# Hybrid mLSTM and stick-breaking layer: k's turned blocks sent by GpSimd, q's weight multiplied on landing, one more head with a longer way from split to product

## The chip, the cores and the metric

The kernel runs on one core of a Trainium2 chip. Times are device microseconds of one execution; several runs are made and their median is compared. The engines named below are PE (TensorE: matmuls), DVE (VectorE), ACT (ScalarE), POOL (GpSimd) and SP (SyncE, which here only issues DMAs). Each engine works through its own instructions in order, and an instruction that has to wait holds everything behind it on that engine.

## What is computed

One layer for 512 tokens of width 1024, in float32. The input is normalised and goes through one projection whose columns feed an mLSTM branch (4 heads of 256), a stick-breaking attention branch (8 heads of 128) and the gates; both branches are projected, merged and projected again.

```
h    = rmsnorm(x, norm_w)
proj = h @ w_in + b_in
mq, mk, mv, mi, mf, mo, mz, sq, sk, sv, sz, gates = split(proj)
hm   = mlstm_chunkwise(silu(conv(mq)), silu(conv(mk)), mv, mi, log_sigmoid(mf))
y_m  = rmsnorm(hm) * sigmoid(mo) * silu(mz)
y_s  = stick_breaking_attention(rmsnorm(sq), rmsnorm(sk), sv) * silu(sz)
x    = x + (g_m * (y_m @ w_proj_m) + g_s * (y_s @ w_proj_s)) @ w_out
```

The change lies in the stick-breaking branch. For a block of 128 queries, with z = q k / sqrt(128):

```
log_beta = log_sigmoid(z);  log_1mb = where(causal, log_sigmoid(-z), 0)
between  = reverse_cumsum(log_1mb) - log_1mb
a        = where(causal, exp(log_beta + between), 0)
out      = a @ v
```

## The kernel before

**Units.** The dense products are cut into 118 units; a unit is one piece of a weight of 128 x 1024 numbers and, in most, 24 matmuls of 512 columns. Each float32 operand is split into a high part (ACT copies it to a reduced format) and a low part (DVE subtracts, line 97), and three matmuls (lines 91 to 93) replace one. The main loop (line 1246) goes from unit to unit. In a unit c it runs what was put off to c (`defer`), evacuates the accumulator of unit c - 1, splits weights until two units ahead (`AHEAD`), issues half of the unit's matmuls (`mm(0)`), lets each active attention head take one step (`next(g)`), starts the heads that are due, and issues the other half (`mm(1)`). In the units in `REST` (11, 16, 20, 23, 24, 32, 44, 64) the active heads take no step. There is no scheduler: the order on every engine is the order in which this loop writes.

**The units around the change.** Set 1 of the stick-breaking heads has q in units 16 to 19, k in 20 to 23, z in 24 to 27, v in 28 to 31. The first mLSTM pair follows: its output gate in 32 to 35, its z in 36 to 39, its q and k with the convolution in 40 to 47, its v in 48 to 51. A v group fills four PSUM banks (`dps`), all that there are for dense units; unit 32 can begin once DVE has taken the first of them out (line 413). The z evacuation has two DVE instructions (690, 691), a convolution four (702, 704) with a sigmoid on ACT (707), a multiply (710) and a last subtraction (719).

**Turned blocks.** Where (q or k, set) stands in `TURNED`, the 32x32 blocks of the raw rows are transposed by DVE (`turn`, tile `ty`), and in the next unit 16 DMAs (`move`, line 399) put the blocks at their places (tile `tz`, one for each pair of heads). In set 1 every second one of the 16 is issued by POOL, the others by SP. q's rows are not scaled by its norm weight before; `head` multiplies the whole tile by the weight vector `qkw` (line 434) ahead of the split of each even head.

**A head** (`head`, line 424) is a generator; each `yield` ends a step. Step 1 splits q and k (`qtt`, `ktt`). Step 2 makes the scores of rows 3, 0 and 1 on PE and weighs rows 3 and 0: two sigmoids on ACT, two masks on POOL (463, 466), a scan and a product on DVE (469, 470). Step 3 makes the scores of row 2, transposes the blocks of rows 3 and 0 (487) and weighs rows 1 and 2. Step 4 transposes the rest. Steps 5 and 6 issue 8 DMAs each (line 506, by POOL in set 1) that put the blocks in place (`az`, two buffers). Step 7 is empty. Step 8 splits the first two columns of blocks (`ath`, `atl`: `turn((0,))`, `turn((1,))`), step 9 multiplies them with v (`apply`) and splits the other two (`turn((2, 3))`), step 10 multiplies these, step 11 multiplies the result by the gate (546). In set 1 the heads 2 and 3 take one empty step before each of the two products.

`SB_START` holds the unit in which each head takes its first step: 30, 33, 35 and 38 for set 1. So head 0 makes its scores in 31, head 2 in 36, head 3 in 39; head 0's last split stands in 39, head 1's in 41 with its product in 42.

Of the kernel before, what the change touches and what calls it, by code (L numbers as in the profile page):

```python
# [9 lines left out]
FR = mybir.dt.float32r  # L10
BF = mybir.dt.bfloat16
AF = mybir.ActivationFunctionType
OP = mybir.AluOpType
# [10 lines left out]

SB_START = [10, 13, 16, 19, 30, 33, 35, 38]
M_START = [52, 56, 70, 76]
GATES_PREP, GATES_START = 3, 4
TURNED = {("q", 0), ("q", 1), ("k", 1)}  # L30
# [5 lines left out]
def tile_hybrid_layer(  # L36
# [16 lines left out]
    nc = tc.nc  # L53
# [20 lines left out]
    def blk(tag, dt=F32, shape=(512,), name=None, p=128):  # L74

        where = mp if tag in MISC else sp
        return where.tile([p] + list(shape), dt, name=name or tag, tag=tag, bufs=BUFS[tag])

    def two(tag, dt=F32, name=None):

        t = blk(tag, dt, (2, 512), name=name)
        return t[:, 0, :], t[:, 1, :]
# [4 lines left out]
    def att_ps():  # L87
        return psa.tile([128, 512], F32, name="aps", tag="aps")
# [6 lines left out]
    def split(src, hi, lo):  # L95
        nc.scalar.activation(hi, src, AF.Copy)  # L96
        nc.vector.tensor_tensor(lo, src, hi.bitcast(F32), op=OP.subtract)  # L97
# [98 lines left out]
    def defer(n, fn):  # L196
        later.setdefault(now[0] + n, []).append(fn)
# [26 lines left out]
    qkw = cst.tile([128, 1], F32, name="qkw")  # L224
# [93 lines left out]
    class SbSet:  # L318
# [64 lines left out]
        def turn(self, name, g):  # L383

            ty = sp.tile([128, 8, TB, 32], F32, name="ty", tag="A", bufs=4)
            for tb in range(TB):
                nc.vector.transpose(ty[:, :, tb, :],
                                    self.raw[name][tb][:, 256 * g:256 * g + 256].rearrange("p (x j) -> p x j", j=32))  # L390

            def move():
                tz = blk("qk", F32, (2, 4, 128), name="tz")
                self.tz[name].append(tz)
                src = ty.rearrange("p (h b) i j -> p b h (i j)", h=2)
                for b in range(4):
                    for a in range(4):
                        q = nc.gpsimd if self.s and a % 2 else nc.sync
                        q.dma_start(tz[32 * b:32 * b + 32, :, a, :], src[32 * a:32 * a + 32, b])

            defer(1, move)
            if g == 0:
                defer(1 if name == "k" else 2, lambda: self.turn(name, 1))
            elif name == "k":
                defer(3, lambda: done.add(("k", self.s)))
# [18 lines left out]
        def head(self, h):  # L424
            hs = slice(h * 128, (h + 1) * 128)
            tr = []
            for name in ("q", "k"):
                th, tl = own = two("qk", FR, name=name + "tt")
                if (name, self.s) in TURNED:
                    tp = self.tz[name][h // 2][:, h % 2].rearrange("p a (i j) -> p i a j", j=32)  # L430
                    th, tl = [x.rearrange("p (i a j) -> p i a j", a=4, j=32) for x in own]
                    if name == "q" and h % 2 == 0:
                        z = self.tz[name][h // 2]
                        nc.vector.tensor_scalar(z, z, qkw, None, op0=OP.mult)
                else:
                    tp = att_ps()
                    for tb in range(TB):
                        nc.tensor.transpose(tp[:, tb * 128:(tb + 1) * 128], self.raw[name][tb][:, hs], ident)
                if name == "q" and not (name, self.s) in TURNED:
                    nc.scalar.activation(th, tp, AF.Copy, scale=qkw)  # L440
                    nc.vector.scalar_tensor_tensor(tl, tp, qkw, th.bitcast(F32), op0=OP.mult, op1=OP.subtract)
                else:
                    split(tp, th, tl)
                tr.append(own)
# [58 lines left out]
            for b in range(4):  # L503
                for a in range(4):
                    q = nc.gpsimd if self.s else nc.sync
# [9 lines left out]
            def turn(js):  # L515
                n0, n1 = slot[js[0], js[0]], slot[TB - 1, js[-1]] + 1
                at = (n1 - n0) * 128
                ah, al = blk("y", FR, name="ath"), blk("y", FR, name="atl")
                split(az[:, :, n0:n1, :].rearrange("p b i j -> p i b j"),
                      *[x[:, 0:at].rearrange("p (i b j) -> p i b j", b=4, j=32) for x in (ah, al)])  # L520
                for j in js:
                    o, n = (slot[j, j] - n0) * 128, T - j * 128
                    a_parts[j] = ah[:, o:o + n], al[:, o:o + n]

            turn((0,))
            turn((1,))
            yield
            if self.s and h >= 2:
                yield
            op = att_ps()  # L530

# [4 lines left out]
            apply(0)  # L536
            apply(1)
            turn((2, 3))
            yield
            if self.s and h >= 2:  # L540
                yield
            apply(2)
            apply(3)
# [1 line left out]
            y = y_s[4 * self.s + h]  # L545
# [668 lines left out]
    for s in (0, 1):  # L1214
        for h in range(4):
            pend.append((SB_START[4 * s + h], 1,
                         lambda s=s: ("k", s) in done, lambda s=s, h=h: sets[s].head(h)))
# [28 lines left out]
    for c in range(N):  # L1246
# [26 lines left out]
        for e in list(pend):  # L1273
            if c >= e[0] and e[2]():
                pend.remove(e)
                g = e[3]()
# [36 lines left out]
```

## Time and profile before

| what | value |
|---|---|
| median of 3 runs | 703.98 us (702.88 to 704.81) |
| profiled execution, its own time | 703.04 us |
| span of the profiled execution | 701.3 us |
| mean granted clock of TensorE over the span | 0.997 |
| POOL busy | 156.1 us, 22% |
| SP's queue (q1): share of 16 DMA engines | 37.0% |
| POOL's queue (q0): share of 16 DMA engines | 6.3% |

The page gives the busy time of each engine and its share of the span. A list of waits gives, for an engine, the instruction that waited and what it waited for. A timeline row has the start from the span's beginning, the duration, the engine, the line, the operation and its tiles, and in brackets the idle time of the engine before it with what ended that. A table by stretches has the stretch and its length, then the busy time and number of instructions of PE, of its weight loads, of DVE, ACT and POOL, then the granted clock of TensorE, the share of the DMA engines and GB/s. The matmuls are pipelined, so their durations overlap; their pace is read from start to start.

### The profile page before, as it was taken

Reading aid. Unit: us, or ns where it says so; the run is one execution under the profiler, and the core shown is the slowest. Engines: PE = TensorE matmul, PEld = TensorE weight load, DVE = VectorE, ACT = ScalarE, POOL = GpSimd, SP = SyncE. Lnnn points to the kernel's source line nnn. Section 1 sums busy time; section 2 is a strip of 40 time slices with the busy share of each in tenths; the row PEclk is TensorE's granted clock in tenths of the full one; section 3 lists DMA queues with packets and bytes.
Section 4 is the critical chain, followed back from the end, with each engine's and each line's share of the span. In section 5 each row is a group of like instructions: output and inputs, shape, how many; then the busy total and the mean of one; then the engine's idle time right before and its main releaser. Section 6 shows DMA issues by size and latency. Waiting matters only on the chain.

```text
span 701.3 us, 9357 instructions
## 1 busy us (share of the span) xinstructions
PE 688.5 (98%) x3172; PEld 571.2 (81%) x3172; DVE 472.9 (67%) x835; ACT 334.6 (48%) x629; POOL 156.1 (22%) x345
## 2 busy tenths in 40 slices
PE   7999999999999999899999999999999999999997
PEld 5888888788887788788888888888888888888886
DVE  6847997866847797998634638995444364445896
ACT  6244364565335554344365534447464353344451
POOL 5422132265602666400002020001111000111010
PEclk9999999999999999999999999999999999999999
DMA  7433524535553343333342244433323446589334
GB/s 246 136 89 103 164 71 125 142 84 164 147 162 91 98 128 98 101 90 104 90 100 82 60 104 125 118 91 90 91 61 83 113 150 225 140 171 225 127 80 131
DMA packets 109881, 84.11 MB, mean 120 GB/s; under 512 B 8302, under 2 KB 92680, under 8 KB 109832
## 3 DMA queue, kind: packets, MB, share of 16 engines
q1 hardware_dynamic: 104600, 73.93, 37.0%
q0 software_dynamic: 5088, 9.44, 6.3%
q8 instruction: 25, 0.41, 0.2%
q14 instruction: 24, 0.20, 0.1%
q10 hardware_dynamic: 144, 0.13, 0.1%
HBM read 65.12 MB, written 2.10 MB: 96 GB/s over the span
## 4 chain that ended last, share of the span: by engine, by line
PE 88%; DVE 5%; POOL 3%; DMA 1%; issue 1%; ACT 1%; SPq 1%; DVEq 0%; POOLq 0%; ACTq 0%
PE dps L91 25%; PE dps L93 25%; PE dps L92 25%; PE aps L92 3%; PE aps L93 3%; PE aps L91 2%; POOL az L506 1%; PE dps L1202 1%; DVE wl L97 1%; PE dps L1200 1%; PE dps L1201 1%; DMA stg<-in_w_in_dram 1%; PE aps L812 1%; PE aps L814 1%; DVE om L469 1%
## 5 line engine op out<-in xcount | busy, mean ns | idle before, releaser
L97 DVE TENSOR_TENSOR wl<-stg,wh 128x1024 fp32r<-128x1024 f32 x92 | 112.5, 1223 | 111.4 <-ACT wh L96 110.3
L91 PE MATMUL dps<-hh,wh 128*128 128x512 f32 x448 | 175.8, 392 | 1.3 <-DVE tmp L413 1.3
L93 PE MATMUL dps<-hh,wl 128*128 128x512 f32 x448 | 175.0, 391 | 0.0
L92 PE MATMUL dps<-hl,wh 128*128 128x512 f32 x448 | 174.9, 390 | 0.0
L96 ACT ACTIVATE wh<-stg 128x1024 fp32r<-128x1024 f32 x92 | 96.7, 1052 | 56.8 <-PE dps L93 28.0
L91 PEld LDWEIGHTS dps<-hh,wh 128*128 128x128 f32 x448 | 84.6, 189 | 18.3 <-DVE tmp L413 1.7
L93 PEld LDWEIGHTS dps<-hh,wl 128*128 128x128 f32 x448 | 84.4, 188 | 18.0
L92 PEld LDWEIGHTS dps<-hl,wh 128*128 128x128 f32 x448 | 84.5, 189 | 16.8
L91 PE MATMUL dps<-wh,hh 128*128 128x512 f32 x224 | 88.2, 394 | 0.4 <-DVE qraw L346 0.4
L93 PE MATMUL dps<-wh,hl 128*128 128x512 f32 x224 | 87.3, 390 | 0.0
L92 PE MATMUL dps<-wl,hh 128*128 128x512 f32 x224 | 87.3, 390 | 0.0
L91 PEld LDWEIGHTS dps<-wh,hh 128*128 128x128 f32 x224 | 42.1, 188 | 9.3 <-issue 0.8
L93 PEld LDWEIGHTS dps<-wh,hl 128*128 128x128 f32 x224 | 42.0, 188 | 9.0
L92 PEld LDWEIGHTS dps<-wl,hh 128*128 128x128 f32 x224 | 42.1, 188 | 8.2
L704 DVE SCALAR_TENSOR_TENSOR acc<-tmp,vec,acc 128x511 f32<-128x511 f32 (+2 forms) x48 | 36.0, 750 | 1.7
L707 ACT ACTIVATE tmp<-acc 128x512 f32<-128x512 f32 x16 | 10.1, 633 | 56.5 <-DVE acc L704 56.5
L463 POOL TENSOR_SCALAR_AFFINE_SELECT om<-om 128x128 f32<-128x128 f32 x32 | 17.3, 541 | 85.5 <-ACT om L461 85.5
L506 POOL DMA_DIRECT2D az<-ay x64 | 31.8, 504 | 19.7 <-ACT tmp L699 11.3
L469 DVE TENSOR_TENSOR_SCAN om<-om 128x512 f32<-128x512 f32 (+3 forms) x32 | 26.8, 836 | 9.2 <-POOL om L463 9.1
L125 POOL DMA_DIRECT2D wl<-stg x8 | 6.9, 868 | 93.7 <-DVE yml L97 61.7
L765 POOL TENSOR_SCALAR_AFFINE_SELECT w_all<-om 128x128 f32<-128x128 f32 x16 | 5.1, 351 | 91.7 <-DVE om L760 91.7
L461 ACT ACTIVATE om<-aps,rq 128x512 f32<-128x512 f32 (+3 forms) x32 | 16.8, 525 | 17.4 <-PE aps L93 16.5
(276 smaller groups left out, 1281.6 us busy)
## 6 DMA issues: line engine op xcount, KB each, us to landing
stg<-in_w_in_dram SPq DMA_DIRECT2D x87, 512.0 KB, 3.8
stg<-in_w_proj_s_dram SPq DMA_DIRECT2D x8, 512.0 KB, 3.9
B<-in_w_out_dram SPq DMA_DIRECT2D x8, 512.0 KB, 4.7
stg<-in_w_proj_m_dram SPq DMA_DIRECT2D x8, 512.0 KB, 3.7
wl<-stg POOLq DMA_DIRECT2D x8, 512.0 KB, 5.8
az<-ay SPq DMA_DIRECT2D x64, 40.0 KB, 2.7
az<-ay POOLq DMA_DIRECT2D x64, 40.0 KB, 1.8
brow<-in_b_in_dram SPq DMA_DIRECT2D x8, 256.0 KB, 5.5
```

The costliest lines, as they stand in the source:

```text
L91: nc.tensor.matmul(ps, ah, bh, start=first, stop=False)
L92: nc.tensor.matmul(ps, ah, bl, start=False, stop=False)
L93: nc.tensor.matmul(ps, al, bh, start=False, stop=last)
L96: nc.scalar.activation(hi, src, AF.Copy)
L97: nc.vector.tensor_tensor(lo, src, hi.bitcast(F32), op=OP.subtract)
L461: nc.scalar.activation(om[:, 0:n], zp, AF.Sigmoid, scale=rn[:, h:h + 1])
L463: nc.gpsimd.affine_select(out=om[:, ts], in_=om[:, ts], compare_op=OP.is_gt, fill=1.0, base=0, channel_multiplier=1, pattern=[[-1, 128]])
L469: nc.vector.tensor_tensor_scan(back, back, back, 1.0, op0=OP.mult, op1=OP.bypass)
L506: q.dma_start(az[32 * a:32 * a + 32, b, :, :], ay[32 * b:32 * b + 32, a, :, :])
L704: nc.vector.scalar_tensor_tensor(acc[:, j:], t[:, 0:T - j], cw(3 - j, ch), acc[:, j:], op0=OP.mult, op1=OP.add)
L707: nc.scalar.activation(t, acc, AF.Sigmoid)
L812: nc.tensor.matmul(nm[:, 0:258], ph, vh, start=j == 0, stop=False)
```

## The change

Five edits, all in the stick-breaking branch. The starts of heads 0, 1 and 2 of set 1 go one unit later. All 16 transfers of a turned k tile of set 1 are issued by POOL; q's stay shared. The multiply by q's weight leaves `head` and is put off to the third unit after the turn, when the transfers of the tile (issued in the first) are under way or landed. In set 1 head 1 too gets an empty step before each product. And the last split of a head of set 1 takes its tiles from the pool `qk` (tile name `at2`) and not from `y`.

```diff
-SB_START = [10, 13, 16, 19, 30, 33, 35, 38]
+SB_START = [10, 13, 16, 19, 31, 34, 36, 38]
@@ turn
-                        q = nc.gpsimd if self.s and a % 2 else nc.sync
+                        q = nc.gpsimd if self.s and (name == "k" or a % 2) else nc.sync
                         q.dma_start(tz[32 * b:32 * b + 32, :, a, :], src[32 * a:32 * a + 32, b])
+            def weight():
+                z = self.tz[name][g]
+                nc.vector.tensor_scalar(z, z, qkw, None, op0=OP.mult)
+
             defer(1, move)
+            if name == "q":
+                defer(3, weight)
@@ head
-                    if name == "q" and h % 2 == 0:
-                        z = self.tz[name][h // 2]
-                        nc.vector.tensor_scalar(z, z, qkw, None, op0=OP.mult)
@@ head, turn(js)
-                ah, al = blk("y", FR, name="ath"), blk("y", FR, name="atl")
+                if self.s and js == (2, 3):
+                    ah, al = two("qk", FR, name="at2")
+                else:
+                    ah, al = blk("y", FR, name="ath"), blk("y", FR, name="atl")
@@ head, before apply(0) and before apply(2)
-            if self.s and h >= 2:
+            if self.s and h >= 1:
                 yield
```

With the rest units the steps of set 1 now fall so: head 0 makes its scores in 33, its last split in 40 and that product in 41; head 1 its last split in 43 and the product in 46; head 2 its scores in 37, its last split in 46 and the product in 48. Head 3's steps stay where they were. The lines below 399 are six higher or so in the changed kernel (413 is 419, 469 is 472, 506 is 509, 707 is 713).

Three places in the order of the engines. DVE around the evacuation of set 1's v, in units 30 to 32 (wl: a weight's low part; tz: the weight multiply; om and a_all: head 0's scans and products; tmp<-dps: the evacuation), before:

```order
L97 TENSOR_TENSOR wl<-stg,wh 128x1024
L97 TENSOR_TENSOR atl<-az,ath 128x384
L434 TENSOR_SCALAR tz<-tz,qkw 128x1024
L97 TENSOR_TENSOR qtt<-tz,qtt 128x512
L97 TENSOR_TENSOR ktt<-tz,ktt 128x512
L97 TENSOR_TENSOR wl<-stg,wh 128x1024
L469 SCALAR_TENSOR_TENSOR om<-om 128x512
L470 TENSOR_TENSOR a_all<-a_all,om 128x512
L469 SCALAR_TENSOR_TENSOR om<-om 128x128
L470 TENSOR_TENSOR a_all<-a_all,om 128x128
L413 TENSOR_TENSOR tmp<-dps,brow 128x512 x2
```

and now:

```order
L97 TENSOR_TENSOR wl<-stg,wh 128x1024
L97 TENSOR_TENSOR atl<-az,ath 128x384
L97 TENSOR_TENSOR wl<-stg,wh 128x1024
L97 TENSOR_TENSOR qtt<-tz,qtt 128x512
L97 TENSOR_TENSOR ktt<-tz,ktt 128x512
L419 TENSOR_TENSOR tmp<-dps,brow 128x512 x2
```

The two scans and their products have gone behind the evacuation, and the multiply has left the place; the splits of head 0 now stand directly ahead of the evacuation.

ACT from the weight's high part of unit 40 to that of unit 42 (ath<-az 128x384, and in the changed kernel the tile numbered at_2906: a head's last split, or the second of its first two; tmp<-acc: the sigmoid of a convolution; om and a_all: head 3's rows 1 and 2), before:

```order
L96 ACTIVATE wh<-stg 128x1024
L96 ACTIVATE ath<-az 128x512
L96 ACTIVATE ath<-az 128x384
L461 ACTIVATE om<-aps,rq 128x256
L465 ACTIVATE a_all<-aps,rq 128x256
L461 ACTIVATE om<-aps,rq 128x384
L465 ACTIVATE a_all<-aps,rq 128x384
L96 ACTIVATE wh<-stg 128x1024
L699 ACTIVATE tmp<-dps,bvec 128x512
L707 ACTIVATE tmp<-acc 128x512
L96 ACTIVATE ath<-az 128x384
L96 ACTIVATE wh<-stg 128x1024
```

and now:

```order
L96 ACTIVATE wh<-stg 128x1024
L96 ACTIVATE at_2906<-az 128x384
L464 ACTIVATE om<-aps,rq 128x256
L468 ACTIVATE a_all<-aps,rq 128x256
L464 ACTIVATE om<-aps,rq 128x384
L468 ACTIVATE a_all<-aps,rq 128x384
L96 ACTIVATE wh<-stg 128x1024
L705 ACTIVATE tmp<-dps,bvec 128x512
L713 ACTIVATE tmp<-acc 128x512
L96 ACTIVATE ath<-az 128x512
L96 ACTIVATE ath<-az 128x384
L96 ACTIVATE wh<-stg 128x1024
```

Head 0's last split stands ahead of the sigmoid of the first convolution; behind it, where head 1's last split stood, are now head 1's first two splits.

POOL in units 39 and 40 (az<-ay: the blocks of a head, eight issues a step; om and a_all: head 3's masks), before, from the issues of units 38 and 39 on:

```order
L506 DMA az<-ay 32x320 x16
L462 MEMSET om 128x1
L463 AFFINE_SELECT om<-om 128x128
L466 AFFINE_SELECT a_all<-a_all 128x128
L462 MEMSET om 128x1
L463 AFFINE_SELECT om<-om 128x128
L466 AFFINE_SELECT a_all<-a_all 128x128
L506 DMA az<-ay 32x320 x8
```

and now, from those of unit 39 on:

```order
L509 DMA az<-ay 32x320 x8
L465 MEMSET om 128x1
L466 AFFINE_SELECT om<-om 128x128
L469 AFFINE_SELECT a_all<-a_all 128x128
L465 MEMSET om 128x1
L466 AFFINE_SELECT om<-om 128x128
L469 AFFINE_SELECT a_all<-a_all 128x128
L509 DMA az<-ay 32x320 x8
```

The first eight issues of head 2 came ahead of the masks of head 3's rows 3 and 0; they now come behind them and ahead of those of its rows 1 and 2. They wait for the last split of head 0, since `az` has two buffers.

More of the change, by code (lines that the diff above doesn't have):

```diff
@@ L539, in head @@
             yield
-            if self.s and h >= 2:
+            if self.s and h >= 1:
                 yield
```

## The prediction

> **What bounds the kernel now.** The page comes first: the busy line of TensorE (PE) against the span.
>
> ```profile
> span 701.3 us, 9357 instructions
> ...
> PE 688.5 (98%) x3172; PEld 571.2 (81%) x3172; DVE 472.9 (67%) x835; ACT 334.6 (48%) x629; POOL 156.1 (22%) x345
> ```
>
> PE is busy for 688.5 of 701.3 us. The change takes no matmul away and adds none, so it can win only from the pauses of PE, 12.8 us, and from stretches at a lower clock. The second view is PE's list of waits (who waited for what: total, times, longest); these are the ones that lie in the stretch that the change touches.
>
> ```profile
> PE aps L91 <- ACT ath L96: 1.8, 1, 1.8
> ...
> PE dps L91 <- DVE tmp L413: 1.3, 1, 1.3
> ...
> PE aps L91 <- ACT ktt L96: 0.6, 1, 0.6
> ...
> PE aps L92 <- DVE ktt L97: 0.3, 1, 0.3
> ```
>
> Each comes once. The timeline says where, and what it costs in starts of matmuls (start, duration, instruction, idle before it); the unit is found by counting 24 dense matmuls for each. First the evacuation of v, between units 31 and 32.
>
> ```profile
> 214.33 0.39 PE L93 MATMUL dps<-wh,hl 128*128 128x512 f32 x1
> 216.00 0.50 PE L91 MATMUL dps<-hh,wh 128*128 128x512 f32 x1 [1.29 <-DVE tmp L413]
> ```
>
> Matmuls with 512 columns otherwise start 0.23 apart (242.76 to 242.99 just below), so this one costs 1.67 - 0.23 = 1.44 us. VectorE (DVE) at the same place:
>
> ```profile
> 212.39 1.23 DVE L469 TENSOR_TENSOR_SCAN om<-om 128x512 f32<-128x512 f32 x1 [1.64 <-POOL om L463]
> ...
> 215.26 1.28 DVE L413 TENSOR_TENSOR tmp<-dps,brow 128x512 f32<-128x512 f32 x2
> ```
>
> The scans of head 0 (set 1) stand ahead of L413 in DVE's order and hold it until 215.26. Next the scores of head 2, in unit 36, with DVE and ScalarE (ACT) ahead of them:
>
> ```profile
> 242.76 0.39 PE L92 MATMUL dps<-hl,wh 128*128 128x512 f32 x1
> 242.99 0.39 PE L93 MATMUL dps<-hh,wl 128*128 128x512 f32 x1
> ...
> 244.74 0.50 PE L92 MATMUL aps<-ktt,qtt 128*128 128x512 f32 x1 [0.30 <-DVE ktt L97]
> ```
>
> ```profile
> 241.95 0.75 DVE L434 TENSOR_SCALAR tz<-tz,qkw 128x1024 f32<-128x1024 f32 x1
> ...
> 243.39 0.69 DVE L97 TENSOR_TENSOR qtt<-tz,qtt 128x512 fp32r<-128x512 f32 x1 [0.70 <-ACT qtt L96]
> 244.00 0.68 DVE L97 TENSOR_TENSOR ktt<-tz,ktt 128x512 fp32r<-128x512 f32 x1
> ```
>
> Two starts, 1.75 apart from 242.99 to 244.74 where 0.46 is normal: 1.29 us. The chain is the weight multiply (L434), then ACT's split that waits for it, then DVE's two subtractions; from 241.95 to 243.39 DVE does only the multiply and waits. The third pause is the product of head 1 in unit 42:
>
> ```profile
> 284.11 0.39 PE L93 MATMUL dps<-hh,wl 128*128 128x512 f32 x1
> 286.31 0.38 PE L91 MATMUL aps<-ath,vh 128*128 128x256 f32 x1 [1.81 <-ACT ath L96]
> 286.90 0.43 PE L92 MATMUL aps<-atl,vh 128*128 128x256 f32 x1 [0.21 <-DVE atl L97]
> ```
>
> ```profile
> 282.22 0.54 DVE L702 TENSOR_SCALAR acc<-tmp,vec 128x512 f32<-128x512 f32 x1
> ```
>
> ```profile
> 285.21 0.63 ACT L707 ACTIVATE tmp<-acc 128x512 f32<-128x512 f32 x1 [8.66 <-DVE acc L704]
> 285.75 0.51 ACT L96 ACTIVATE ath<-az 128x384 fp32r<-128x384 f32 x1
> ```
>
> Two starts take 2.79 where 0.23 + 0.11 is normal: 2.45 us. The split of head 1 (ath, 285.75) stood on ACT behind the sigmoid of the first convolution (L707) (8.66 idle), which waited for DVE's convolution, begun only at 282.22. The busy table of the stretch right after shows a second price (PE first, PEclk third from the right), beside the stretches after the other two pauses:
>
> ```profile
> 216.00:221.58 5.58, 5.58 (x25) 4.61 (x25) 4.91 (x8) 3.43 (x5) 0.00 (x0) 1.00 0.01 3
> 240.49:248.73 8.24, 7.38 (x34) 5.68 (x33) 6.69 (x13) 4.45 (x8) 5.95 (x16) 1.00 0.34 91
> 287.40:290.80 3.40, 3.40 (x12) 2.79 (x12) 3.36 (x7) 1.01 (x2) 2.40 (x5) 0.54 0.11 28
> ```
>
> The granted clock is 0.54 for 3.40 us: 0.46 x 3.40 = 1.6 us lost. The waits at 216 and 243 brought no such drop.
>
> **The change part by part.** The base is the profiled execution, 703.04 us (span 701.3 and 1.7 around it); the median of the runs shown, 703.98, lies 0.9 above it.
>
> Removed, later start of head 0 (unit 31, scores in 33 because 32 is a rest unit): its scans now stand behind L413, so unit 32 finds its bank free: -1.44. What is late next is the splits of head 0, which now stand ahead of L413; they have all of the first half of unit 31.
>
> Removed, weight multiply ahead of head 2's split: 0.75 for the multiply and 0.70 of DVE's wait for ACT are gone, ACT can split as soon as it is free. DVE then begins qtt at 241.95 and ends ktt near 243.2; PE wants it at 243.45. So -1.29, with 0.2 to spare.
>
> Moved, the multiply itself: four of 0.75, in the units 8, 10, 25 and 27 instead of 10, 16, 30 and 36. It adds a wait on DVE for the 16 transfers; queued behind it are the k rows and the next weight's low part, which have two units. Hidden; if the cover were gone, at most 0.75 each, 3 in all.
>
> Moved, 16 transfers of k from SP to GpSimd (POOL). Eight issues on POOL and the first use of k:
>
> ```profile
> 181.54 4.21 POOL L399 DMA_DIRECT2D tz<-ty  x8 [2.46 <-DVE ty L389]
> ```
>
> ```profile
> 207.93 0.62 ACT L96 ACTIVATE ktt<-tz 128x512 fp32r<-128x512 f32 x1
> ```
>
> Thirty-two issues take 4 x 4.21 = 16.8 us from 181.5, to 198.4, and the first 16 are out at 190; head 0 needs only those, in unit 31 at 207. POOL's next work there is the selects behind head 0's scores. Cost and gain 0: SP issues weight loads earlier, and no wait of PE names one of them.
>
> Added, two units between split and product for head 1, and its tile from another pool: the split of head 0's last columns now stands in unit 40, ahead of the convolution, and its product in 41; head 1's stands in 43 with its product in 46. So -2.45, and with it the half clock, -1.6.
>
> Sum of what goes: 1.44 + 1.29 + 2.45 + 1.6 = **6.8 us**.
>
> Against it stands DVE, which was given time by these pauses. I carry its queue on by steps measured here:
>
> ```profile
> 247.58 1.22 DVE L469 TENSOR_TENSOR_SCAN om<-om 128x512 f32<-128x512 f32 x1
> ...
> 250.24 0.75 DVE L690 SCALAR_TENSOR_TENSOR tmp<-dps,bvec,tmp 128x512 f32<-128x512 f32 x1
> ...
> 251.69 1.31 DVE L97 TENSOR_TENSOR wl<-stg,wh 128x1024 fp32r<-128x1024 f32 x1
> 252.92 1.07 DVE L487 STREAM_TRANSPOSE ay<-a_all 128x128 f32<-128x128 f32 x5
> 253.92 0.64 DVE L469 TENSOR_TENSOR_SCAN om<-om 128x256 f32<-128x256 f32 x1
> ...
> 256.54 0.74 DVE L690 SCALAR_TENSOR_TENSOR tmp<-dps,bvec,tmp 128x512 f32<-128x512 f32 x1
> ```
>
> ```profile
> 234.49:240.49 6.00, 6.00 (x28) 5.03 (x27) 4.41 (x12) 3.42 (x6) 6.00 (x16) 1.00 0.46 115
> 194.88:200.32 5.44, 5.44 (x26) 4.51 (x24) 2.89 (x4) 2.00 (x3) 0.00 (x0) 1.00 0.19 50
> 302.81:309.49 6.68, 6.68 (x32) 5.59 (x31) 6.12 (x9) 2.67 (x4) 0.00 (x0) 1.00 0.33 86
> ```
>
> From start to start: rows 3 and 0 of a head 2.66, evacuation of z 1.45, low part of a weight 1.23, five transposes 1.00, rows 1 and 2 2.62, splits of a head 1.2. A unit of PE is 5.44 bare, 6.00 with one score block, 6.68 with scores or a product. Zero is the start of unit 36, which repeats unit 35 of before (234.49); DVE is at 241.95 - 234.49 = 7.5, and at 8.7 after head 2's splits. Unit 37: 8.7 + 1.45 + 1.23 + 1.00 + 2.66 = 15.0. Unit 38: + 1.45 + 1.23 + 1.00 + 2.62 + 1.2 = 22.5, the end of head 3's splits. PE begins unit 39 at 6.00 + 6.68 + 6.00 = 18.7 and wants them 2.9 later, at 21.6: a **new wait of 0.9** at head 3's scores, because heads 2 and 3 are now two units apart and not three.
>
> In unit 40 a hold comes that before has in unit 39:
>
> ```profile
> 264.95 0.55 DVE L97 TENSOR_TENSOR atl<-az,ath 128x384 fp32r<-128x384 f32 x1
> ...
> 270.07 1.29 DVE L469 TENSOR_TENSOR_SCAN om<-om 128x512 f32<-128x512 f32 x1 [4.57 <-POOL om L463]
> ```
>
> POOL may issue head 2's blocks only when the last split of head 0 is done (265.5), and head 3's selects stand behind these issues: DVE waits 4.6. From there on each unit of DVE is a convolution, 5.16 long (rows below; 0.6 multiply, 1.2 low part of a weight, 2.8 convolution, 0.6 last subtraction):
>
> ```profile
> 294.72 0.68 DVE L710 SCALAR_TENSOR_TENSOR tmp<-acc,tmp 128x512 f32<-128x512 f32 x1
> ...
> 299.88 0.68 DVE L546 TENSOR_TENSOR ys<-aps,ys 128x512 f32<-128x512 f32 x1
> ```
>
> PE, with unit 39 at 6.68 + 0.9, begins units 40 to 46 at 26.3, 33.5, 39.5, 44.9, 51.6, 57.0 and 62.5 (7.2 for product and score block together, 6.0, 5.44, 6.68, 5.44, 5.44). DVE: unit 39, 22.5 + 1.45 + 1.23 + 1.1 (two splits of head 0) + 1.0 + 2.66 = 29.9. Unit 40, + 1.45 + 1.23 + 0.5 (its last split) = 33.1, hold 4.6, scans 2.6: 40.3. Unit 41, + 4.0 (no multiply and last subtraction yet) + 2.3 (sigmoid 0.63 and two splits of 0.51 on ACT, then 0.55 here) + 1.0 = 47.6. Unit 42, + 5.16 + 0.6 = 53.4. Unit 43, + 5.16 + 1.2 (ACT) + 1.65 (three splits) = 61.4. In unit 44 the low part of unit 46's weight ends 1.8 later, at 63.2, where PE wants it at 62.7: **0.5 late**. The same steps on to unit 48 put head 2's last split and head 3's first about 0.5 behind their products.
>
> New waits: 0.9 + 0.5 + 0.5 = 1.9, between 0 (steps 5% shorter, some 2 us by unit 44) and 4 (5% longer). The forecast is 703.0 - 6.8 + 1.9 = **698.1 us**.
>
> Of the half clock, the Trainium skill ("TensorE: Matmul & The Clock Gate", section "HAM oscillation — how this bites in real kernels") gives the rule that PE's gaps must stay below about 3.4 us. The trace disagrees: waits of 1.81 and 0.21, with two short matmuls between, were followed by 0.54. By that rule the drop would not hang on this wait and would stay, the time being 1.6 higher.
>
> **The rivals.** (B) The half clock does not hang on the wait and comes again elsewhere. For it: 1.29 of waiting at 216 brought none. Against it: it begins within a us of the longest wait. 698.1 + 1.6 = 699.7. (C) L413 stays late: head 0's splits now stand ahead of it, behind the low part of a weight whose load may be late. 698.1 + 1.4 = 699.5. Against it: SP is relieved just before. (D) DVE's backlog brings one long wait back in units 42 to 48, with its half clock: 698.1 + 2.45 + 1.6 = 702.2. (E) Slower: the hold on POOL in unit 40. In my sum the low parts for units 44 and 45 end at 49.4 and 55.2, 2.4 and 2.0 before PE wants them; if head 0's last split, and with it POOL's issue, head 3's selects and DVE's scans, come more than 2 us later than I have, PE waits in 44, 45 and 46 in turn, and two such waits with their half clock give 698.1 + 2 x 4.05 = 706.2.
>
> **How the numbers follow.** Forecast 57%, B 10%, C 10%, D 15%, E 8%. A measurement of this kernel can tell about 0.3% (2.1 us) from no change. The forecast, B and C are faster by more: 0.77; D is within it of 703.98: 0.15; E is slower: 0.08. The range goes from no new wait, 703.0 - 6.8 with the rounding, 696.0, to D, 702.2, and leaves out E and little else.
>
> **What would show it.** Right: no wait of PE for L413's successor or ahead of head 2's scores, no granted clock of 0.54 after 284, PE's waits now at head 3's scores (unit 39, for ktt on DVE) and for a weight's low part near unit 46; k's transfers on POOL only, done before 200. Wrong: a wait over 2 us in units 40 to 48, a stretch at half clock, POOL's issue of head 2's blocks far behind unit 40, or L413 still late at unit 32.

## The result, and the profile after

The change made the kernel **slower**: 705.70 us (median of 10 runs, 704.45 to 706.67) against 703.13 of before in the same comparison; ratio 1.0033, 95% interval 1.0023 to 1.0042. A second comparison gave 1.0033 again (1.0021 to 1.0045). The forecast was 698.1, in a range from 696.0 to 702.2. Executions at a low clock throughout, such as one of 761.93 us at a clock of 0.851 further down, count in no ratio.

The page and TensorE's (PE's) list of waits of the changed kernel, in the columns of before:

```profile
span 704.9 us, 9367 instructions
...
PE 691.1 (98%) x3172; PEld 574.0 (81%) x3172; DVE 472.4 (67%) x835; ACT 334.9 (48%) x629; POOL 166.0 (24%) x361
```

```profile
PE dps L91 <- ACT tmp L705: 4.4, 1, 4.4
...
PE aps L92 <- DVE ktt L97: 0.4, 1, 0.4
...
PE aps L441 <- DVE kraw L368: 0.3, 1, 0.3
PE aps L92 <- DVE at L97: 0.2, 1, 0.2
```

Every pause that was to go is gone: L413's successor, head 2's scores and head 1's product stand in no row. (The row on `ktt` is head 3's scores, at 261.70, and the row on `at` head 2's product, at 318.33.) The busy table has no idle PE and no lower clock in units 32 and 36, in unit 43, and in unit 46, where head 1's product now stands (PE's busy time first, PEclk third from the right):

```profile
214.28:219.72 5.44, 5.44 (x25) 4.51 (x24) 4.15 (x6) 2.21 (x3) 0.00 (x0) 1.00 0.01 3
```

```profile
239.39:245.39 6.00, 6.00 (x29) 5.03 (x27) 4.39 (x11) 4.46 (x8) 6.00 (x17) 1.00 0.44 113
```

```profile
284.56:291.24 6.68, 6.68 (x31) 5.59 (x30) 6.22 (x13) 2.90 (x5) 0.00 (x0) 1.00 0.18 47
```

```profile
302.12:309.52 7.40, 7.40 (x37) 6.30 (x36) 6.81 (x10) 2.68 (x4) 5.67 (x12) 1.00 0.55 143
```

In their place is a wait that before did not have, 4.4 us for the evacuation L705. The timeline places it at the second half of unit 48, with VectorE (DVE) and ScalarE (ACT) ahead of it:

```profile
326.25 0.79 PE L91 MATMUL dps<-wh,hh 128*128 128x512 f32 x1 [4.42 <-ACT tmp L705]
```

```profile
324.05 0.63 ACT L713 ACTIVATE tmp<-acc 128x512 f32<-128x512 f32 x1 [3.38 <-DVE acc L710]
324.58 1.04 ACT L96 ACTIVATE wh<-stg 128x1024 fp32r<-128x1024 f32 x1
325.53 0.67 ACT L705 ACTIVATE tmp<-dps,bvec 128x512 f32<-128x512 f32 x1
```

```profile
321.05 0.54 DVE L708 TENSOR_SCALAR acc<-tmp,vec 128x512 f32<-128x512 f32 x1
321.63 2.32 DVE L710 SCALAR_TENSOR_TENSOR acc<-tmp,vec,acc 128x511 f32<-128x511 f32 x3
```

Unit 48 is the first of v for the mLSTM, a group by tokens: one unit fills all four banks of `dps`. Its last bank is that of unit 47, whose evacuation (L705, 325.53) stands on ACT behind the sigmoid of unit 46 (L713), and this waits for DVE's convolution of unit 46, begun at 321.05, 6.1 us after PE began unit 48 (314.96). PE had finished unit 47 long before. Behind the wait comes a half clock:

```profile
326.20:331.60 5.40, 5.35 (x13) 4.19 (x14) 4.72 (x8) 1.56 (x3) 0.00 (x0) 0.50 0.50 146
331.60:335.00 3.40, 3.40 (x16) 2.79 (x15) 2.38 (x4) 1.58 (x2) 0.00 (x0) 1.00 0.02 5
```

0.50 of 5.40 us is 2.7 us lost. (The half clock is granted for 6.8 us, from 324.8 on; in the first 1.4 of them PE still waits.) The starts of units keep the books of the two profiled executions:

| from - to | before | after | difference |
|---|---|---|---|
| start to unit 30 | 200.32 | 201.43 | +1.1 (0.5 of it unit 10) |
| unit 30 to 48 | 120.78 | 113.53 | -7.25 |
| units 48 and 49 | 12.30 | 20.73 | +8.4 |
| unit 50 to the issue of the last store | 364.79 | 364.80 | 0.0 |
| that issue to the end of the span | 3.1 | 4.4 | +1.3 |

The gain came, and more was given back in two units; and 1.3 us came where nobody looked, behind the issue of the last store.

```profile
698.19 0.37 ACTq L1077 DMA_DIRECT2D out_dram<-xr  x1
```

```profile
700.49 0.37 ACTq L1083 DMA_DIRECT2D out_dram<-xr  x1
```

These are the issues of the last store, before (span 701.3) and after (span 704.9).

### The profile page after: what moved, and what is told of

Read it like the earlier page. It is cut to its first block, busy times and chain, and to the rows that moved or that the text cites. A ratio compares the mean times of both kernels' runs of the same rounds, so it can differ in the third digit from the quotient of the medians.

```text
span 704.9 us, 9367 instructions
## 1 busy us (share of the span) xinstructions
PE 691.1 (98%) x3172; PEld 574.0 (81%) x3172; DVE 472.4 (67%) x835; ACT 334.9 (48%) x629; POOL 166.0 (24%) x361
## 4 chain that ended last, share of the span: by engine, by line
PE 59%; issue 12%; DVE 9%; DMA 6%; POOL 3%; ACT 1%; SPq 0%; DVEq 0%; POOLq 0%; ACTq 0%
PE dps L91 17%; PE dps L93 17%; PE dps L92 17%; DVE acc L710 2%; DMA wl<-stg 2%; POOL az L509 2%; PE aps L92 2%; PE aps L93 2%; PE aps L91 2%; DVE wl L97 1%; DMA az<-ay 1%; DMA xr<-u 1%; DMA stg<-in_w_proj_m_dram 1%; DMA xr<-in_x_dram 1%; DVE om L472 1%
## 5 line engine op out<-in xcount | busy, mean ns | idle before, releaser
L713 ACT ACTIVATE tmp<-acc 128x512 f32<-128x512 f32 x16 | 10.1, 633 | 57.3 <-DVE acc L710 57.3
L399 POOL DMA_DIRECT2D tz<-ty x48 | 25.9, 549 | 5.0 <-DVE ty L389 2.4
```

The lines of the kernel that those rows point to most:

```text
L713: nc.scalar.activation(t, acc, AF.Sigmoid)
```

## The experiments

**Theory 1**: from unit 36 to 48 the bound is DVE, with ACT in its train; PE's early pauses were time given to DVE, and without them PE arrives earlier at a place that DVE reaches no earlier. **Theory 2**: GpSimd (POOL), which issues head 3's blocks behind head 1's last split, sets unit 48. **Theory 4**: the transfers of k hold POOL. **Theory 5** came later, for the 1.3 us at the end. (The numbers are those of the expectations; there is no theory 3.)

### Less work for VectorE, and the same work earlier

One of the convolution's four taps, a multiply-add, left out (so the kernel no longer computes the layer), on the changed kernel:

```
-                for j in (1, 2, 3):
+                for j in (1, 2):
```

> The changed kernel with one of the convolution's four taps left out (the multiply-add of j=3, so the output is not the reference's): VectorE has 0.76 us less to do in each of the 16 convolutions, 7 of which lie before unit 48. Theory 1 (VectorE is behind, and ScalarE's evacuation of unit 47 stands behind the sigmoid that waits for the convolution): the 4.4 us wait of the matmul of v (L91, for tmp of L705) falls below 0.5, the stretch at granted clock 0.5 behind it goes, unit 48 takes about 9 instead of 14 us, and the time is 698.5 (706.65 less 4.4, 2.6 and about 1). Theory 2 (the lateness comes from GpSimd, which issues head 3's blocks only when head 1's last split is done): the tap changes little of it, the wait stays over 2 us and the time above 703.

Measured: 698.35 us, ratio 0.9937 (0.9922 to 0.9952). No wait at unit 48 (it takes 7.40 us), no half clock. Seven convolutions by 0.76 are 5.3 us, the units begin 0.7 earlier from the start on, and the evacuation of unit 47 is issued 6.2 us earlier, at 319.33. As theory 1 had it.

Next, the hold of DVE that the prediction had seen in unit 40, taken away by the order of two heads' steps. The hold,

```profile
276.78 0.76 DVE L472 TENSOR_TENSOR_SCAN om<-om 128x256 f32<-128x256 f32 x1 [3.62 <-POOL om L466]
```

(a row of the changed kernel), with this edit:

```
-        for g in list(act):
+        for g in (act[:2] + act[3:] + act[2:3] if c == 40 else list(act)):
```

> The changed kernel with head 3's step ahead of head 2's in unit 40 only, so that GpSimd makes head 3's masks before it issues head 2's blocks; nothing else is changed. Theory 1: the hold of VectorE in unit 40 (3.6 us, scan for om of GpSimd) goes; VectorE stands 3.6 us less behind in unit 48, the 4.4 us wait there shrinks to about 0.8, and the half clock with it: 706.65 - 3.6 - 2.6 = 700.5. Theory 2 (GpSimd's later issue, of head 3's blocks behind head 1's last split, sets unit 48): the wait at unit 48 stays within 1 us of 4.4 and the time within 1 us of 706.6.

Measured: 700.06, ratio 0.9959 (0.9946 to 0.9971). The hold is gone, DVE is 4.1 us earlier (convolution of unit 46 at 316.96), and unit 48 waits 1.40, with no half clock:

```profile
322.15 0.50 PE L91 MATMUL dps<-wh,hh 128*128 128x512 f32 x1 [1.40 <-ACT tmp L705]
```

Theory 2 expected 4.4 and 706.6. But POOL's issue of head 3's blocks, behind head 1's last split, moved by as much as DVE (295.27 for 299.38), so this run alone does not part the two; the one with the sigmoid below does.

The same edit on the kernel before, in unit 39 (`c == 39`):

> The kernel before with head 3's step ahead of head 2's in unit 39 only, so that GpSimd makes head 3's masks before it issues head 2's blocks (VectorE's hold of 4.6 us there goes). Theory 1 (VectorE's lateness is what TensorE pays for, at whichever place comes first): the 1.8 us wait at head 1's product in unit 42 and the half clock behind it go, though nothing of the change is in; time 703.0 - 2.0 - 1.6 = 699.4. Rival (the wait at head 1's product stands on its own, for the split stands behind the sigmoid whatever VectorE did before): the wait stays, time within 0.5 of 703.0.

Measured: 701.45, ratio 0.9975 (0.9966 to 0.9984): a miss by 2 us, and the most telling one. The 1.81 at head 1's product and the half clock are gone as theory 1 says. But PE, now at unit 48 at 317.62 instead of 321.10, waits there:

```profile
PE dps L91 <- ACT tmp L699: 1.4, 1, 1.4
```

I had not applied my own theory a second time: what PE wins ahead of unit 48 it pays at unit 48 as soon as DVE is the later one.

### The parts of the change, one by one

Without the further unit for head 1 (`h >= 2` again in both places), on the changed kernel:

> The changed kernel without the further unit between split and product for head 1 (heads 2 and 3 keep theirs, as before). Theory 1 (the pause is only moved): the pause stands at head 1's product again, about 3 to 5 us with a half clock behind it, in unit 43 or 44; with that given to VectorE, the 4.4 us wait of unit 48 is gone; the time is within 2 us of the changed kernel's 706.6. The rival, that the added unit (and its tile from the pool of q and k) is the whole loss: the pauses of unit 48 go and none comes in their place, time 699.

Measured: 703.68, ratio 1.0015 (1.0006 to 1.0024). The pause is back at head 1's product, 2.92 us with a half clock of 3.4 us behind it, and unit 48 has none, though the evacuation of unit 47 is issued when it was:

```profile
284.37 0.51 PE L91 MATMUL aps<-ath,vh 128*128 128x512 f32 x1 [2.92 <-ACT ath L96]
```

```profile
325.07 0.67 ACT L705 ACTIVATE tmp<-dps,bvec 128x512 f32<-128x512 f32 x1
```

PE paused for DVE at unit 42 instead of unit 48. The rival, a loss by the unit itself, expected 699.

The weight on landing alone, on the kernel before:

> The kernel before with q's weight multiplied on landing and nothing else of the change. The term of the prediction: head 2's scores in unit 36 lose their 1.29 us; in unit 10 a transpose now waits 0.33 for k's scaling. If VectorE's time is what counts (theory 1), the pause of head 1's product in unit 42 grows by about what unit 36 gave, since VectorE gets no work done in the pauses that are gone: about 1 us back, time 703 within 0.5. If the pauses are independent of one another, as the prediction added them up, the time is 702.0 (703.0 - 1.29 + 0.33).

Measured: 701.55, ratio 0.9984 (0.9975 to 0.9993), better than both expectations. The 1.29 of unit 36 is gone, unit 10 pays 0.5, and head 1's pause did not grow (1.56 for 1.81, with no half clock behind it). DVE is earlier too: it begins the first convolution at 280.57 and not at 282.22, since in unit 36 it has neither the multiply of 0.75 nor the 0.70 of waiting for ACT. Unit 48 now waits 1.43. So a pause in which DVE itself waits, or does work that can stand elsewhere, is a gain for DVE and PE alike; theory 1 in the form "pauses are DVE's time" was too strong.

Head 1's further unit and its tile alone, on the kernel before (the diff's lines on `h >= 1` and on `at2`):

> The kernel before with head 1's further units between split and product (and its tile from the pool of q and k) and nothing else of the change. If pauses add up one by one: the 2.45 us at head 1's product and the half clock of 1.6 go, 703.1 - 4.05 = 699.0. Theory 1: they go, but the evacuation of unit 47 stays within 1 us of 325.7 on ScalarE, where TensorE now wants it about 4 us earlier than before, at about 323.5: a wait of 2 to 3 us at unit 48 (L91, for tmp of L699), with a half clock behind it if it is over 2: 701.4 without, 704.0 with it.

Measured: 702.93, ratio 1.0010 (0.9996 to 1.0024). As theory 1 had it: the pause is gone at unit 42 and stands at unit 48, with 2.73 us, the evacuation at 324.36:

```profile
325.08 0.50 PE L91 MATMUL dps<-wh,hh 128*128 128x512 f32 x1 [2.73 <-ACT tmp L702]
```

The ten runs part by their granted clock: those at 0.999 and 1.000 took 701.47 to 701.96, those at 0.993 and 0.995 took 704.54 to 706.00, and the three between, at 0.997 and 0.998, 702.66 to 704.04. The one profiled is among the first and has no half clock behind the wait. So the half clock seems to come after this wait in some runs and not in others, and to cost some 3.5 us; that is read from the mean clocks, for no run with it was profiled.

The later starts alone, on the kernel before (`SB_START` 31, 34, 36, 38 in set 1):

> The kernel before with the later starts of heads 0, 1 and 2 of set 1 and nothing else of the change. If pauses add up one by one, as in the prediction: the 1.44 us at L413 goes and nothing comes for it, 703.1 - 1.4 = 701.7. Theory 1 (a pause of TensorE ahead of unit 48 is VectorE's time; taken away it comes back later): the 1.29 at L413 goes, the wait at head 1's product grows beyond its 1.8 to about 3, the half clock stays, time 703.2 (as the changed kernel without head 1's further unit, 703.7, less the 0.5 of unit 10).

Measured: 709.97, ratio 1.0111 (1.0095 to 1.0126): both forecasts wrong. The wait at head 1's product has grown to 2.91, as theory 1 had it, but PE waits another 4.21 in unit 48. DVE and ACT lose 5 us there:

```profile
323.46 0.52 ACT L96 ACTIVATE ath<-az 128x384 fp32r<-128x384 f32 x1 [5.24 <-PE aps L92]
```

The split of head 3 waits for a product of PE. With one unit less between heads 2 and 3 their splits meet, which asks for more tiles of the pool `y` than are free. In the changed kernel the tile `at2` avoids this. To show it, the starts together with that tile:

> The kernel before with the later starts of heads 0, 1 and 2 and with the last splits of a head of set 1 in a tile from the pool of q and k; no further unit for head 1, the weight and k's transfers as before. If the later starts alone lost through the tiles (head 3's split on ScalarE waited 5.24 us in unit 48 for a tile that head 2's product still read), this wait is gone, the evacuation of unit 47 is issued near 325 and not at 330.7, and the time is 710.0 - 5 - 1 = 703.5 to 704 (as the changed kernel without head 1's further unit, 703.7, less 1.3 at the end and 0.5 of unit 10, plus the multiply). If not, 709 to 710 again.

Measured: 703.55, ratio 1.0005 (0.9996 to 1.0014), both waits in unit 48 gone, the evacuation at 325.91. The line on `at2`, which looks like a detail of the further unit, is worth some 7 us beside the starts (1.0111 against 1.0005).

### ScalarE's order

On the changed kernel, unit 46's sigmoid behind unit 47's evacuation (`hold` is unit 46; `self.sig` is then called in unit 47's evacuation, behind L705):

```
+                if hold:
+                    self.prev()
...
-                self.prev()
-                nc.scalar.activation(t, acc, AF.Sigmoid)
+                if not hold:
+                    self.prev()
+                    nc.scalar.activation(t, acc, AF.Sigmoid)
...
+                    def sig():
+                        nc.scalar.activation(t, acc, AF.Sigmoid)
+                        mult()
```

> The changed kernel, with one sigmoid moved: that of unit 46 is issued on ScalarE behind the evacuation of unit 47 instead of ahead of it (its multiply goes with it, and the low part of unit 45's block stands ahead of unit 46's convolution on VectorE, so that the buffer is free). VectorE has as much to do as before and is as late. Theory 1 in its full form (VectorE's lateness reaches TensorE only because the evacuation stands behind that sigmoid on ScalarE): the 4.4 us wait at unit 48 shrinks to about 0.9, no half clock follows, time 706.65 - 3.5 - 2.6 = 700.5, though VectorE's convolutions begin within 1 us of where they did. Rival (the lateness of VectorE reaches TensorE in any case, through a weight's low part or a tile): the wait comes back at unit 48 or 49 with over 2 us, time above 704.

Measured: 699.74, ratio 0.9951 (0.9935 to 0.9968). The profile read below is of one further run:

> The changed kernel with unit 46's sigmoid behind unit 47's evacuation once more, for a profile of an undisturbed execution. Theory 1 in its full form: VectorE's convolution of unit 46 begins within 1 us of the changed kernel's 321.05, the evacuation of unit 47 is issued about 3.5 us earlier than its 325.53, the wait at unit 48 is 0.9 or less, no half clock; 699.7. Rival: VectorE's convolution is earlier too, so that the order on ScalarE has little to do with it.

Measured: 699.40 in one run. DVE is as late as before, and PE hardly waits:

```profile
320.61 0.54 DVE L713 TENSOR_SCALAR acc<-tmp,vec 128x512 f32<-128x512 f32 x1
```

```profile
320.78 0.69 ACT L705 ACTIVATE tmp<-dps,bvec 128x512 f32<-128x512 f32 x1 [0.21 <-DVE mkt L731]
```

```profile
321.52 0.51 PE L91 MATMUL dps<-wh,hh 128*128 128x512 f32 x1 [0.72 <-ACT tmp L705]
```

POOL's issue of head 3's blocks is as late as in the changed kernel too (298.35, PE 1.0 ahead, for 299.38), so theory 2 falls. Lateness of DVE alone costs little at unit 48; it reaches PE through one instruction on ACT that stands ahead of another for no need.

The books of all these, from the profiled executions (us):

| kernel | PE begins unit 48 | unit 47's evacuation issued | PE waits in unit 48 |
|---|---|---|---|
| before | 321.10 | 325.73 | 0 |
| changed | 314.96 | 325.53 | 4.42 |
| changed, no unit for head 1 | 319.73 | 325.07 | 0 |
| before, unit for head 1 | 316.87 | 324.36 | 2.73 |
| before, weight on landing | 317.86 | 324.05 | 1.43 |
| before, order in unit 39 | 317.62 | 323.81 | 1.43 |
| changed, order in unit 40 | 314.56 | 321.43 | 1.40 |
| changed, sigmoid behind | 313.96 | 320.78 | 0.72 |
| changed, a tap less | 314.26 | 319.33 | 0 |

Between before and changed PE moved by 6.1 us and the evacuation by 0.2. That is why the gain ahead of unit 48 came back as a wait; the half clock behind it and the end of the program add the rest.

### The end of the program

k's transfers shared again, on the changed kernel (`a % 2` for both names):

> The changed kernel with the transfers of k's turned blocks of set 1 shared between SyncE and GpSimd again, as before the change. Theory 1: no wait of TensorE hangs on them, the time stays at 706.6 within 1 us, and the 4.4 us wait at unit 48 is there unchanged. Theory 4 (GpSimd is held by the 16 further issues and everything behind it is late): the wait at unit 48 falls by over 2 us and the time below 704.

Measured: 704.70, ratio 1.0023 (1.0013 to 1.0032). The wait at unit 48 is there with 4.40, so theory 4 falls; but the time is lower, by 0.7 us by the ratios (1.0023 for 1.0033; their intervals overlap). The stretch from the last store's issue to the end is 3.1 us here, and 4.3 to 4.5 in the kernels so far with k's transfers on POOL (but for one profile, named below). Hence theory 5, with k's transfers alone on the kernel before:

> The kernel before with k's transfers of set 1 all on GpSimd and nothing else of the change. The prediction's term: no gain and no loss, 702.9 as before on this chip. Theory 5 (the 16 further transfers on GpSimd lengthen the end of the program): the stretch from the issue of the last store to the end of the span grows from 3.1 to about 4.4 us, no unit begins later than before by over 0.3 for it, time +1.3, ratio 1.0018.

Measured: 704.46, ratio 1.0018 (1.0009 to 1.0027), no unit later than before, and a last store issued at the same time, with a span of 702.6:

```profile
698.17 0.37 ACTq L1077 DMA_DIRECT2D out_dram<-xr  x1
```

As expected. And the other way:

> The kernel before with all of q's and k's transfers of set 1 on SyncE, none on GpSimd. If the end of the program grows with each transfer on GpSimd, by 1.3 us for 16 or 32, it shrinks from 3.1 to about 1.8 us or less, time 701.5. If 3.1 is what the end takes without any backlog, it stays at 3.1 and the time at 702.9 or, where SyncE's weight loads come late behind the transfers, above it.

Measured: 718.43, ratio 1.0217 (1.0203 to 1.0230). The end is 3.3 us and doesn't shrink. The reason stands in rows that the timeline leaves out, those of the line that closes the program. Each engine has drains there. POOL's first is long and begins at its last transfer; SP's are short and come once the last store has landed (700.2 before). The three numbers are the shortest, middle and longest in ns, the times those of the first and the last start. First the kernel before, then the changed one, then this one:

```profile
L1309 POOLq DRAIN  x3: 40/98/10222, 690.3 to 701.1; - x3
L1309 SPq DRAIN  x3: 7/7/7, 700.5 to 700.8; - x3
```

```profile
L1315 POOLq DRAIN  x3: 40/98/11533, 692.6 to 704.7; - x3
L1315 SPq DRAIN  x3: 7/7/7, 702.9 to 704.4; - x3
```

```profile
L1309 POOLq DRAIN  x3: 40/98/8790, 705.4 to 716.5; - x3
L1309 SPq DRAIN  x3: 7/7/7, 715.9 to 716.2; - x3
```

POOL's long drain takes 10.2 us where POOL issues 110 transfers in the program (as before), 11.5 with 126 (as changed) and 8.8 with 78 (here), the same to 0.01 us in all twenty profiled executions. The program ends 0.8 us after the later of POOL and SP. Before, both are done at 700.5, by chance; in the changed kernel POOL is done at 704.1, 1.1 after SP; here at 714.2, 1.7 before SP. So the 16 further transfers make POOL's drain 1.3 us longer, and all but 0.2 of that stands out behind SP's end; the 32 fewer shorten a drain that SP's end then hides. The one profile with k's transfers on POOL and an end of only 3.3 us (the first of the kernel with the sigmoid behind) has the 11.5 too, but its last store is issued 9.0 us after POOL's last transfer, where the others have 7.8 to 8.0. The 15 us are another matter: on SyncE (SP) the weight loads and heads' blocks stand behind k's and q's transfers, and a unit's split waits 12.83 for its weight:

```profile
203.10 1.06 ACT L96 ACTIVATE wh<-stg 128x1024 fp32r<-128x1024 f32 x1 [12.83 <-DMA stg<-in_w_in_dram]
```

What POOL does in its drain no view shows; it stays open.

### The half clock

On the changed kernel, matmuls in place of the wait (`fill` is 18 in this group, 0 elsewhere):

```
+                    if g == 0 and tb == 2:
+                        for _ in range(fill):
+                            nc.tensor.matmul(ps[tb], hh[:, 0, 0:128], hh[:, 0, :], start=True, stop=True)
```

> The changed kernel with 18 further matmuls of 512 columns in unit 48, into the bank of the third token block ahead of its own (which start the bank anew, so that nothing of theirs stays): TensorE is busy for 18 x 0.23 = 4.1 of the 4.4 us that it otherwise waits for the evacuation of unit 47; VectorE and ScalarE are not touched. Theory 1 (VectorE's chain sets the end of unit 48, and the half clock behind it is the price of TensorE's idleness alone): unit 48 ends where it did within 1 us, the stretch at granted clock 0.5 goes, time 706.65 - 2.6 = 704.0, ratio to before 0.9996 where the changed kernel has 1.0033. Rival (the half clock comes from something else than idleness): it stays, time 706 to 707.

Measured: 704.64, ratio 1.0024 (1.0013 to 1.0035): not the 2.6 us. So both once more on one chip:

> The changed kernel once more, unchanged, on one chip with the kernel whose wait at unit 48 is filled with matmuls: 705.7, ratio 1.0033, mean granted clock 0.994 to 0.996.

> The changed kernel with 18 matmuls in the wait of unit 48, on one chip with the changed kernel itself. If the half clock costs what the trace shows (0.5 for 5.4 us, 2.6 us) and nothing takes it up later: 2.6 us below the changed kernel. If later pauses take most of it up: about 1 us below, as the first time, with a mean granted clock of 0.998 in the runs all the same.

Measured: 705.32 for the changed kernel, ratio 1.0033 (1.0021 to 1.0045), 704.89 with the fill, 1.0030 (1.0018 to 1.0041). In the traces the half clock is gone (0.60 against 1.00 in this stretch, first the changed kernel, then the fill) and PE's last matmul begins 2.3 us earlier, 696.41 against 698.75:

```profile
326.00:332.00 6.00, 6.00 (x17) 4.72 (x18) 5.08 (x8) 1.63 (x4) 0.00 (x0) 0.60 0.44 131
```

```profile
326.00:332.00 6.00, 6.00 (x27) 4.96 (x28) 5.00 (x8) 1.63 (x4) 0.00 (x0) 1.00 0.46 134
```

So the half clock came of the idleness: filled, the same place has none. But 1.0 of the 2.3 us is lost again at the end, where DVE waits for POOL's accumulating transfer to land:

```profile
686.40 0.69 DVE L1084 TENSOR_TENSOR xr<-aps,xr 128x512 f32<-128x512 f32 x1 [1.49 <-DMA xr<-u]
```

In the kernel before the wait there is 0.32, in the changed kernel on the same chip there is none. Why the landing is later, and why the timed runs keep only 0.4 (the two intervals overlap), is not settled. So the price of a half clock behind unit 48 is open: 2.3 us at PE's end in the traces, 0.4 in these runs, some 3.5 by the clocks of the runs with head 1's unit alone.

### A version that beats both

The order in unit 40, the sigmoid behind, and the weight on landing in set 1 alone, on the changed kernel; then the same with k's transfers shared:

> The changed kernel with head 3 ahead of head 2 in unit 40, unit 46's sigmoid behind unit 47's evacuation, and q's weight multiplied on landing for set 1 only (set 0 as before the change). Theory 1: the 1.4 us that stayed at unit 48 with the order alone goes (1.6 with the matmul's refill), and the 0.33 of unit 10 (0.5 in unit starts): 700.06 - 1.6 - 0.4 = 698.1, the time that the prediction gave. Rival (with TensorE ahead again, VectorE's lateness comes out at the next place, a weight's low part in units 49 to 51): about 700.

> The version with head 3 ahead of head 2 in unit 40, unit 46's sigmoid behind unit 47's evacuation and the weight on landing for set 1 only, with k's transfers shared between SyncE and GpSimd as before the change. Theory 5: the end of the program is 3.1 us again, time 697.9 - 1.3 = 696.6, ratio 0.991. If k's place is worth nothing, 697.9 and 0.9928 as that version.

Measured: 697.91, ratio 0.9928 (0.9915 to 0.9942), and **696.55, ratio 0.9904 (0.9891 to 0.9918)**, both within 0.2 us of what was expected. PE's list of waits has six rows left: four in the first units, one for `qraw` (0.4) and one at head 3's scores (0.4).

## Why the prediction was wrong

**The removals**: right, all of them; units 30 to 48 became 7.25 us shorter, where the sum had 5.4 by then (6.8 less 0.9 and 0.5). Of the 1.85 between, 0.9 are the new waits, which came smaller or not at all, and 0.6 is work that now stands in unit 48, which takes 7.40 us without any wait (a tap less) for 6.84 before.

**The new waits**: head 3's scores cost 0.5 in starts (0.9 forecast), head 2's last split in unit 48 0.48 (0.5 forecast). The low part for unit 46 came in time: it ended at 301.95, which is 62.6 on the prediction's scale, for 63.2.

**The step that failed** is "The same steps on to unit 48 put head 2's last split and head 3's first about 0.5 behind their products". In its place unit 48 had a wait of 4.42 us, 4.6 in starts, and behind it a half clock of 2.7. DVE's queue was carried on rightly as far as it went: it was forecast to be done with unit 43's splits at 61.4, and was at 61.3 (the low part that stands next in unit 44 begins at 300.73, and zero is 239.39). What I asked of it was only weights' low parts and heads' splits, with two units of notice each. I did not carry ACT's queue along, where the evacuation stands behind a sigmoid that waits for the convolution, nor ask which unit needs a bank back at once. Until unit 47 each unit needs one bank of four and a late evacuation costs PE nothing; unit 48 needs four. Behind that lies the sum's form: 6.8 us were added up as if each pause stood alone, while DVE, 6 us behind at its end, had used them.

**The half clock of 1.6** was counted as a gain. It was hardly one in the time. (In the prediction's rows for head 1's product one short matmul stands between the waits of 1.81 and 0.21, at 286.31, and not two.) In the five comparisons the runs of the kernel before at a clock of 0.999 or 1.000 have medians of 703.06, 702.72, 702.26, 703.07 and 703.07 us, those at 0.998 or less 702.90, 703.14, 703.03, 703.16 and 702.91: 0.2 between their means. Ahead of unit 48 a half clock costs nothing, for PE would only wait there; that last is argued from the table above, not shown. Behind unit 48 its price is open, as said above.

**k's transfers at "cost and gain 0"**: wrong, 1.3 us at the end of the program, where POOL's last instruction grew from 10.2 to 11.5 us. The last of them was issued by 201.9 and not by 198.4, which hurt nobody.

**The multiply, "hidden"**: right for set 1; in unit 10 it stands ahead of k's scaling, and unit 10 takes 7.42 us for 6.90.

**The rivals**: D (DVE's backlog brings one long wait back) was the right kind, at 15%, with the wrong place and price: 4.4 + 2.7 and not 2.45 + 1.6, since it was priced as a copy of the wait removed and not from how far DVE would be behind. E had POOL's hold in unit 40 right (3.6 for 4.6) but let it act through low parts.

**The sum of the misses**: forecast -4.9 from the profiled 703.04, measured +3.6, so 8.5 are to be found. The wait in unit 48 with its refill 4.6, its half clock 2.7, the end 1.3, unit 10 0.5 and 0.6 in the first units (in which runs of one kernel differ as much) make 9.7; 0.5 for the low part and 0.4 of head 3's scores, forecast and not come, go off: 8.8. The 0.3 too many are not traced.

## What to carry to other kernels

A pause of the busiest engine can be the time in which another catches up: before counting it as a gain, carry that other engine's queue, and those that stand behind it, to the next place where a group takes all buffers at once, and price the wait there. An instruction that waits should not stand ahead of one that frees a buffer for the busy engine. And measure a change part by part: here the weight on landing gains 1.1 us alone, the starts lose 7 to 8 without a tile from another pool and nothing with it, and k's transfers lose 1.3; the whole shows none of it. The 1.3 had to be looked for in the program's closing instructions, where the engine that ends last sets the time.

## What was not expected of the hardware

Sixteen further transfers issued by GpSimd, 500 us before the end, make GpSimd's last instruction 1.3 us longer. Over all kernels here it takes 8.8, 10.2 and 11.5 us with 78, 110 and 126 transfers issued in the program. The time pays what of it lies behind SyncE's end: in ten of the eleven profiled executions with 126 the stretch from the last store's issue to the end is 4.3 to 4.5 us for 3.1, in the eleventh 3.3; with 32 transfers fewer than before it stays at 3.3.

The half clock has no sharp bound in waiting. In the profiled executions none followed 1.40, 1.43 and 1.56 + 0.21 us, none followed 2.73 (the clocks of other runs of that kernel suggest that it came there), and one followed 1.81 + 0.21 and 4.42. The same wait can go either way: 2.92 + 0.22 brought a half clock without head 1's unit, and 2.91 + 0.22 at the same product brought none in the kernel with the later starts alone. Behind these waits it lasted 3.4 us (1.81 and 2.92) or 6.8 (4.42). The rule cited in the prediction (the Trainium skill, "TensorE: Matmul & The Clock Gate", section "HAM oscillation — how this bites in real kernels"), that gaps stay below about 3.4 us, does not hold here: the 1.81 and the 2.92 lie below it, and the clock was lost all the same.
